# Attention diagonal from products, sample rows in one transpose, last squares by TensorE, conv taps in other proportions

## The chip, the cores and the metric

The kernel runs on one core of a Trainium2 chip. A core has TensorE (PE, with its weight load PEld), VectorE (DVE), ScalarE (ACT), GpSimd (POOL) and SyncE (SP), which issues most of the transfers. The metric is the device time of one launch in microseconds (us).

## What is computed

Two layers of a decoder trunk, for 256 prompt positions and 8 sample positions that share the weights; all in float32.

```python
for l in range(DEPTH):                                  # 2 layers, D_MODEL = 2048
    h = rmsnorm(x, norm_mix[l])
    z = h @ w_in[l]                                     # a_x a_b a_c q k v r lr c_glu d_uv
    ya = a_b * causal_dwconv(a_c * a_x, past_a, conv_a_w)              # 3 taps
    o, S = gla_chunked(q, k, v, log_a, s0)              # gated linear attention, 4 heads
    yb = rms_per_head(o) * gla_norm * silu(r)
    cc = causal_dwconv(c1 * sigmoid(c2), past_c, conv_c_w)             # 31 taps
    yc = silu(layernorm(cc + conv_c_b))
    yd = gelu(u) * (W_s @ layernorm(gelu(vd)) + sg_b)   # chunks of 128 positions
    x = x + concat(ya, yb, yc, yd) @ w_o[l]
    x = x + (silu(n @ w_gate) * (n @ w_up)) @ w_down    # n = rmsnorm(x, norm_ffn[l])
return rmsnorm(x, norm_final), new states

# inside gla_chunked, for positions i >= j of a chunk, b the running sum of log_a:
att[i, j] = sum_d q[i, d] * k[j, d] * exp(b[i, d] - b[j, d])
# on the diagonal the decay is 1:  att[i, i] = sum_d q[i, d] * k[i, d]
```

## The kernel before

All activations are held transposed: features on the partitions, the 264 tokens (256 prompt, 8 sample) along the free side. Every large product goes through `stream` (lines 273 to 324). It reads a weight block of 512 columns in steps of two 128-row tiles. In each step one transfer brings `raw`, ACT rounds it to `wh` (line 293), DVE subtracts to get the remainder `wl` (line 294), and PE makes three products per tile and column group: `wh` by the high half of the activation (line 308), `wh` by its low half (309), `wl` by the high half (310). That is 24 products a step. `wh` and `wl` have three buffers, `raw` four.

The mixer of a layer runs the streams c2, c1, r, q, v, vd, u, ac, ax, ab of eight steps each, then the output projection `w_o` in four streams of eight steps. `w_o` reads the mixed groups in the order of the table at line 829: 12 to 15 (`uu`, spatial gating), 4 to 7 (`rg`, attention), 8 to 11 (`cc`, the conformer conv), 0 to 3 (`ya`, the short conv). Each group has to be rounded to its `yh` (line 382, or 822 for `ya`) and `yl` (383, 823) before PE can use it.

The conformer conv, 31 taps on four tiles of 128 features, doesn't have a place of its own. Its operations (lines 480 to 485, one first tap on ACT and 31 operations on DVE for each tile) come from a generator. After each `wl` of the streams `step_back` (line 250) adds a rate to an account and issues as many as it holds: 1.5 a step for 16 steps, then 2.5 (line 507). When the generator is empty, `fin_c` normalises `cc` and rounds it. A scheduler then fixes the order of the instructions on each engine.

Between q and v the attention is made: the diagonal (lines 563 to 571) as the full 128 by 128 products of keys and queries, from which a predicated copy with the identity mask `idm` takes the diagonal; then seven levels (578 to 604) of decayed blocks, each with a product `ps_lv` and a predicated copy.

At the end, `finish(g, par)` is called after each of the four streams of the last `w_down`. It multiplies by the final gain (`xg`), transposes back to tokens on the partitions, for three token blocks of 128 (the third, tokens 136 to 263, holds the sample's rows in its last eight), adds the squares up in `acc`, and after the last stream takes the sums over the features with `rms_cols` (229), makes the reciprocal root on DVE (`newton`), scales, and writes the results with `dma` on SP.

Of the kernel before, what the change touches and what calls it, by code (L numbers as in the profile page):

```python
# [11 lines left out]
F32 = mybir.dt.float32  # L12
# [3 lines left out]
AF = mybir.ActivationFunctionType  # L16
ALU = mybir.AluOpType

P = 128
D_MODEL = 2048  # L20
KT = D_MODEL // P
NPT = 256
NS = 8
T = NPT + NS
# [21 lines left out]
def hybrid_trunk_kernel(  # L46
# [8 lines left out]
    nc = tc.nc  # L55
# [11 lines left out]
    def psm(name, shape=(P, 512)):  # L67
        t = ps_m.tile([P, 512], F32, tag="m", name=name)
        return t
# [5 lines left out]
    mm = nc.tensor.matmul  # L75
# [10 lines left out]
    nc.gpsimd.memset(ones_g, 1.0 / GW)  # L86
    ones_s = cst.tile([P, P], F32, tag="ones_s", name="ones_s")
    nc.gpsimd.memset(ones_s, 1.0)
    LEVELS = [64, 32, 16, 8, 4, 2, 1]
    idm = cst.tile([P, P], U8, tag="idm", name="idm")  # L90
    smask = cst.tile([P, 4], U8, tag="smask", name="smask")
# [106 lines left out]
    def rstd_cols(cols, n, inv=1.0):  # L198

        hv, y, t = (tmp.tile([P, 12], F32, tag=a, name=a, bufs=2)[:, :n] for a in ("hv", "rs", "nt"))  # L200
        return newton(cols, y, hv, t, inv)
# [27 lines left out]
    def rms_cols(acc):  # L229
        ps = psm("ps_rms")  # L230
        token_means(ps, 0, acc, ones_d)
        return rstd_cols(ps[:, :3], 3)
# [119 lines left out]
    def mixer_phase(l, gain, par, st):  # L352
# [134 lines left out]
        def conv_all():  # L487
            for t in range(4):
                yield from conv_c(t)
# [14 lines left out]
            emit_y(8, cc, tags=("att", "t10"))  # L504

        states_c()
        back.append((conv_all(), fin_c, chain(repeat(1.5, 16), repeat(2.5))))


        rg = mt("rg", [P, 4, T], tag="t4")  # L510
# [46 lines left out]
        def half(r):  # L557
            return slice(r * 64, (r + 1) * 64)

        def blk(Tb):  # L560
            return slice(Tb * P, (Tb + 1) * P)

        for q in range(2):
            for r in range(2):
                pd = psm("ps_dg")
                for Tb in range(2):
                    mm(out=pd[:, blk(Tb)], lhsT=kz[half(r), q, blk(Tb)], rhs=qz[half(r), q, blk(Tb)],
                       start=True, stop=True)
                nc.vector.copy_predicated(
                    out=att[:, 0:2, q, r, :], mask=idm.unsqueeze(1).to_broadcast([P, 2, P]),  # L570
                    data=pd[:, :256].rearrange("p (g i) -> p g i", g=2))

        pma = mt("pm", [P, 4, T])
        pms = [pma[:, 2 * i:2 * i + 2, :NPT] for i in range(2)]
# [251 lines left out]
        win(COL["ab"], 512, ev_ab)  # L826


        order = [o + i for o in (12, 4, 8, 0) for i in range(4)]
        for g in range(4):  # L830
            def ev_o(m, ps, g=g):
                i = 4 * g + m
# [4 lines left out]

    fin = {}

    def fin_tile(g, t, par):  # L840

        if g == 3:
            q = tmp.tile([P, T], F32, tag="t1", name="sqf", bufs=6)
            actf(q, xs[:, 4 * g + t, :], AF.Square)
            tt(out=fin["acc"], in0=fin["acc"], in1=q, op=ALU.add)
        z = tmp.tile([P, T], F32, tag="t1", name="xg", bufs=6)
        ts(out=z, in0=xs[:, 4 * g + t, :], scalar1=par[:, t, ROW["fin"] + g:ROW["fin"] + g + 1],
           scalar2=None, op0=ALU.mult)
        fin.setdefault("xg", []).append(z)

    def finish(g, par):

        if g == 0:
            fin["acc"] = tmp.tile([P, T], F32, tag="acc", name="acc", bufs=1)
            fin["yo"] = act.tile([P, 2, D_MODEL], F32, tag="xl", name="yo")
            fin["ys"] = act.tile([P, D_MODEL], F32, tag="xh", name="ys")
        acc, yo, ys = fin["acc"], fin["yo"], fin["ys"]
        last = g == 3
        if not last:
            add_squares(acc, 2 * g)  # L860
            add_squares(acc, 2 * g + 1)
            for t in range(4):
                fin_tile(g, t, par)
        xg = fin["xg"]
        fin["xg"] = []
        pts = []
        for c in range(3):
            ps = ps_w.tile([P, 512], F32, tag="w", name="ps_y") if last else psm("ps_y")
            for t in range(4):
                transpose(ps[:, t * P:(t + 1) * P], xg[t][:, TOK0[c]:TOK0[c] + P], ident)  # L870
            pts.append(ps)
        if not last:
            for c in range(3):
                dst = yo[:, c, :] if c < 2 else ys
                actf(dst[:, g * 512:(g + 1) * 512], pts[c], AF.Copy)
            return
        y = rms_cols(acc)

        def scaled(c, src, out):
            if c == 1:  # L880
                actf(out, src, AF.Copy, scale=y[:, c:c + 1])
            else:
                ts(out=out, in0=src, scalar1=y[:, c:c + 1], scalar2=None, op0=ALU.mult)

        for c in (0, 1, 2):
            dst = yo[:, c, :] if c < 2 else ys
            for h0, h1 in ((0, 1024), (1024, D_MODEL)):
                if h0:
                    scaled(c, pts[c], dst[:, 1536:])
                hm = min(h1, 1536)  # L890
                scaled(c, dst[:, h0:hm], dst[:, h0:hm])
                if c < 2:
                    dma(out=y_prompt[0, c * P:(c + 1) * P, h0:h1], in_=dst[:, h0:h1])
            if c == 2:
                dma(out=y_sample.rearrange("b s d -> (b s) d"), in_=dst[P - NS:, :])

    def ffn_phase(l, par):
        es = ExitStack()
# [116 lines left out]
```

## Time and profile before

| | us |
|---|---|
| median of 3 runs | 2325.66 (2324.86 to 2325.68) |
| profiled execution | 2325.71 |
| its span, first to last instruction | 2323.8 |
| PE busy | 2293.6 (99%) |
| DVE busy | 1414.0 (61%) |
| ACT busy | 1019.2 (44%) |

The difference between the execution's time and its span, 1.9 us, lies outside the program's instructions. The mean granted clock of TensorE is 0.995 of full speed. The profile's rows name a line, an engine, an operation, and the tiles written and read; buffer numbers are left out. Passes of a float32 product that isn't a transpose appear as two rows each.

### The profile page before, as it was taken

The page shows a single profiled execution, that of the slowest core. Times are in us where ns is not written, and L with a number is a line of the kernel's source. Part 1 is how long each engine was busy: PE and PEld are TensorE (multiplying, and loading weights), DVE is VectorE, ACT ScalarE, POOL GpSimd, SP SyncE. Part 2 cuts the span into 40 slices and gives each one's busy share as a digit, 9 for nine tenths or more (in the row PEclk, how much of TensorE's full clock was granted, in tenths as well). Part 3 has the DMA queues.
Part 4 walks back from the last instruction along what each step waited for, and adds up shares of the span by engine and source line. Part 5 has one row for each costly group of instructions (what it writes and reads, how often), then busy time and mean ns, then how long its engine had stood idle before and what let it go on. Part 6 is the DMA issues. An engine that isn't in the chain of part 4 may idle for free.

```text
span 2323.8 us, 44164 instructions
## 1 busy us (share of the span) xinstructions
PE 2293.6 (99%) x18656; PEld 2271.3 (98%) x18656; DVE 1414.0 (61%) x2076; ACT 1019.2 (44%) x1302; POOL 71.1 (3%) x138
## 2 busy tenths in 40 slices
PE   9999999999999999999999999999999999999997
PEld 8999989999999999999999998999999999999997
DVE  6699966555655555444467998565555555554444
ACT  5644444444444444444345444444444444434333
POOL 3101000000000000000020100000000000000000
PEclk9999999999999999999999999999999999999999
DMA  8446545555555555555574555555555555555553
GB/s 243 146 155 183 172 153 187 182 181 181 180 189 182 182 182 182 179 178 180 182 202 149 174 172 169 162 179 180 181 181 189 182 182 181 182 181 174 177 177 129
DMA packets 208874, 412.44 MB, mean 177 GB/s; under 512 B 14001, under 2 KB 14067, under 8 KB 208644
## 3 DMA queue, kind: packets, MB, share of 16 engines
q1 hardware_dynamic: 204644, 400.53, 54.1%
q0 software_dynamic: 4032, 9.09, 1.5%
q8 instruction: 146, 2.39, 0.4%
q14 instruction: 52, 0.43, 0.1%
HBM read 404.25 MB, written 6.29 MB: 177 GB/s over the span
## 4 chain that ended last, share of the span: by engine, by line
PE 97%; ACT 2%; DVE 0%; issue 0%; DMA 0%; SPq 0%; DVEq 0%; ACTq 0%
PE pw L308 23%; PE pw L309 23%; PE pw L310 23%; PE pwx L308 8%; PE pwx L309 8%; PE pwx L310 8%; PE ps_lv L597 1%; PE ps_os L705 0%; ACT s L701 0%; ACT wh L293 0%; DMA raw<-in_w_in_dram 0%; PE ps_y L870 0%; ACT cc L503 0%; PE ps_sv L774 0%; PE ps_o L667 0%
## 5 line engine op out<-in xcount | busy, mean ns | idle before, releaser
L294 DVE TENSOR_TENSOR wl<-raw,wh 128x1024 fp32r<-128x1024 f32 x752 | 918.8, 1223 | 763.7 <-ACT wh L293 763.0
L293 ACT ACTIVATE wh<-raw 128x1024 fp32r<-128x1024 f32 (+1 forms) x752 | 795.7, 1060 | 1219.5 <-PE pw L309 694.2
L308 PE MATMUL pw<-xh,wh 128*128 128x264 f32 x3136 | 889.4, 286 | 1.9 <-ACT wh L293 1.7
L309 PE MATMUL pw<-xl,wh 128*128 128x264 f32 x3136 | 887.4, 285 | 0.0
L310 PE MATMUL pw<-xh,wl 128*128 128x264 f32 x3136 | 874.0, 285 | 0.1
L308 PEld LDWEIGHTS pw<-xh,wh 128*128 128x128 f32 x3136 | 590.2, 189 | 3.8 <-ACT wh L293 2.4
L309 PEld LDWEIGHTS pw<-xl,wh 128*128 128x128 f32 x3136 | 590.7, 188 | 2.3 <-issue 1.7
L310 PEld LDWEIGHTS pw<-xh,wl 128*128 128x128 f32 x3136 | 583.7, 189 | 6.9 <-issue 4.0
L308 PE MATMUL pwx<-xh,wh 128*128 128x264 f32 x960 | 272.9, 285 | 0.0
L310 PE MATMUL pwx<-xh,wl 128*128 128x264 f32 x960 | 272.2, 284 | 0.0
L309 PE MATMUL pwx<-xl,wh 128*128 128x264 f32 x960 | 272.1, 284 | 0.0
L309 PE MATMUL pw<-hl,wh 128*128 128x264 f32 x880 | 250.6, 285 | 0.0
L308 PE MATMUL pw<-hh,wh 128*128 128x264 f32 x880 | 250.1, 285 | 0.0
L310 PE MATMUL pw<-hh,wl 128*128 128x264 f32 x880 | 248.7, 285 | 0.0
L308 PEld LDWEIGHTS pwx<-xh,wh 128*128 128x128 f32 x960 | 180.8, 188 | 0.1
L310 PEld LDWEIGHTS pwx<-xh,wl 128*128 128x128 f32 x960 | 180.8, 188 | 0.0
L309 PEld LDWEIGHTS pwx<-xl,wh 128*128 128x128 f32 x960 | 180.5, 188 | 0.0
L308 PEld LDWEIGHTS pw<-hh,wh 128*128 128x128 f32 x880 | 165.8, 188 | 0.0
L309 PEld LDWEIGHTS pw<-hl,wh 128*128 128x128 f32 x880 | 165.7, 188 | 0.0
L310 PEld LDWEIGHTS pw<-hh,wl 128*128 128x128 f32 x880 | 165.1, 189 | 0.1
L309 PE MATMUL pwx<-hl,wh 128*128 128x264 f32 x528 | 150.7, 285 | 0.0
L308 PE MATMUL pwx<-hh,wh 128*128 128x264 f32 x528 | 150.2, 285 | 0.0
(311 smaller groups left out, 2259.9 us busy)
## 6 DMA issues: line engine op xcount, KB each, us to landing
raw<-in_w_gate_dram SPq DMA_DIRECT2D x176, 512.0 KB
raw<-in_w_up_dram SPq DMA_DIRECT2D x176, 512.0 KB
raw<-in_w_down_dram SPq DMA_DIRECT2D x176, 512.0 KB
raw<-in_w_in_dram SPq DMA_DIRECT2D x144, 512.0 KB
raw<-in_w_o_dram SPq DMA_DIRECT2D x64, 512.0 KB
raw<-in_w_in_dram SPq DMA_DIRECT2D x16, 528.0 KB
xp<-in_x_prompt_dram SPq DMA_DIRECT2D x4, 512.0 KB
s<-in_state_gla_dram POOLq DMA_DIRECT2D x16, 128.0 KB, 7.9
```

The costliest lines, as they stand in the source:

```text
L293: actf(wh[:, :, :ncol], r[:, :, :ncol], AF.Copy)
L294: sub = tt(out=wl, in0=r[:, :, :512], in1=wh[:, :, :512].bitcast(F32), op=ALU.subtract)
L308: mm(out=o, lhsT=a, rhs=rh[kk], start=first, stop=False)
L309: mm(out=o, lhsT=a, rhs=rl[kk], start=False, stop=False)
L310: mm(out=o, lhsT=wl[:, j, m * P:(m + 1) * P], rhs=rh[kk], start=False, stop=last)
L597: mm(out=pl[:, g * P:(g + 1) * P], lhsT=pm[:, q, blk(Tb)], rhs=qd[:, q, :, Tb * 64:Tb * 64 + 64], start=True, stop=True)
```

## The change

The rates of the conv's operations are 3 a step for eight steps, 2.25 for eight, then 2.5. The projection reads the groups in the order 12, 4, 0, 8. The attention's diagonal is made from a product of queries and keys on DVE (`prod`), summed over each head's 64 features by a narrow product with `ones_r`, and spread by one predicated copy. In `finish` only the two prompt blocks are transposed; the sample's values, 8 tokens by 16 feature tiles, are gathered in one tile `xgs` and transposed once. The squares of the last two tiles are not added on DVE but by products with `one_3` and `ones_d`; for the sample's rows the squares are spread over 16 partitions a token (`accsm`, `sqs`). The results are scaled and written in other pieces.

```diff
@@ -86,6 +86,14 @@
     nc.gpsimd.memset(ones_g, 1.0 / GW)
     ones_s = cst.tile([P, P], F32, tag="ones_s", name="ones_s")
     nc.gpsimd.memset(ones_s, 1.0)
+    one_3 = cst.tile([P, 3], F32, tag="one_3", name="one_3")
+    nc.gpsimd.memset(one_3, 0.0)
+    nc.gpsimd.memset(one_3[:, 0:1], 1.0 / D_MODEL)
+
+    ones_r = cst.tile([P, 2], F32, tag="ones_r", name="ones_r")
+    nc.gpsimd.memset(ones_r, 0.0)
+    for r in range(2):
+        nc.gpsimd.memset(ones_r[r * 64:(r + 1) * 64, r:r + 1], 1.0)
     LEVELS = [64, 32, 16, 8, 4, 2, 1]
     idm = cst.tile([P, P], U8, tag="idm", name="idm")
     smask = cst.tile([P, 4], U8, tag="smask", name="smask")
@@ -504,7 +512,7 @@
             emit_y(8, cc, tags=("att", "t10"))
 
         states_c()
-        back.append((conv_all(), fin_c, chain(repeat(1.5, 16), repeat(2.5))))
+        back.append((conv_all(), fin_c, chain(repeat(3, 8), repeat(2.25, 8), repeat(2.5))))
 
 
         rg = mt("rg", [P, 4, T], tag="t4")
@@ -560,15 +568,16 @@
         def blk(Tb):
             return slice(Tb * P, (Tb + 1) * P)
 
-        for q in range(2):
-            for r in range(2):
-                pd = psm("ps_dg")
-                for Tb in range(2):
-                    mm(out=pd[:, blk(Tb)], lhsT=kz[half(r), q, blk(Tb)], rhs=qz[half(r), q, blk(Tb)],
-                       start=True, stop=True)
-                nc.vector.copy_predicated(
-                    out=att[:, 0:2, q, r, :], mask=idm.unsqueeze(1).to_broadcast([P, 2, P]),
-                    data=pd[:, :256].rearrange("p (g i) -> p g i", g=2))
+        prod = mt("prod", [P, 2, NPT], tag="dd", bufs=2)
+        tt(out=prod, in0=qz[:, :, :NPT], in1=kz[:, :, :NPT], op=ALU.mult)
+        pd = psm("ps_dg")
+        for Tb in range(2):
+            for q in range(2):
+                g = Tb * 2 + q
+                mm(out=pd[:, 2 * g:2 * g + 2], lhsT=prod[:, q, blk(Tb)], rhs=ones_r, start=True, stop=True)
+        nc.vector.copy_predicated(
+            out=att[:, 0:2].rearrange("p s q r i -> p (s q r) i"), mask=idm.unsqueeze(1).to_broadcast([P, 8, P]),
+            data=pd[:, :8].unsqueeze(2).to_broadcast([P, 8, P]))
 
         pma = mt("pm", [P, 4, T])
         pms = [pma[:, 2 * i:2 * i + 2, :NPT] for i in range(2)]
@@ -826,7 +835,7 @@
         win(COL["ab"], 512, ev_ab)
 
 
-        order = [o + i for o in (12, 4, 8, 0) for i in range(4)]
+        order = [o + i for o in (12, 4, 0, 8) for i in range(4)]
         for g in range(4):
             def ev_o(m, ps, g=g):
                 i = 4 * g + m
@@ -837,44 +846,77 @@
 
     fin = {}
 
+    def fin_gain(par, g):
+        return par[:, :, ROW["fin"] + g]
+
+    def spread(a):
+        return a.rearrange("p (s k) -> p s k", s=NS)
+
     def fin_tile(g, t, par):
 
         if g == 3:
             q = tmp.tile([P, T], F32, tag="t1", name="sqf", bufs=6)
             actf(q, xs[:, 4 * g + t, :], AF.Square)
-            tt(out=fin["acc"], in0=fin["acc"], in1=q, op=ALU.add)
+            if t < 2:
+                tt(out=fin["acc"], in0=fin["acc"], in1=q, op=ALU.add)
+            else:
+                qs = tmp.tile([P, T], F32, tag="t1", name="sqs", bufs=6)[:, :P]
+                actf(spread(qs), xs[:, 4 * g + t, NPT:].unsqueeze(2).to_broadcast([P, NS, KT]), AF.Square)
+                fin["sq"].append((q, qs))
         z = tmp.tile([P, T], F32, tag="t1", name="xg", bufs=6)
-        ts(out=z, in0=xs[:, 4 * g + t, :], scalar1=par[:, t, ROW["fin"] + g:ROW["fin"] + g + 1],
+        ts(out=z[:, :NPT], in0=xs[:, 4 * g + t, :NPT], scalar1=fin_gain(par, g)[:, t:t + 1],
            scalar2=None, op0=ALU.mult)
         fin.setdefault("xg", []).append(z)
 
+    def fin_start():
+        fin["sq"] = []
+        fin["acc"] = tmp.tile([P, T], F32, tag="acc", name="acc", bufs=1)
+        fin["yo"] = act.tile([P, 2, D_MODEL], F32, tag="xl", name="yo")
+
+        xh_ = act.tile([P, KT * P], F32, tag="xh", name="xgs")
+        fin["xgs"] = spread(xh_[:, :P])
+        fin["ys"] = xh_[:, P:2 * P]
+
     def finish(g, par):
 
         if g == 0:
-            fin["acc"] = tmp.tile([P, T], F32, tag="acc", name="acc", bufs=1)
-            fin["yo"] = act.tile([P, 2, D_MODEL], F32, tag="xl", name="yo")
-            fin["ys"] = act.tile([P, D_MODEL], F32, tag="xh", name="ys")
-        acc, yo, ys = fin["acc"], fin["yo"], fin["ys"]
+            fin_start()
+        acc, yo, xgs = fin["acc"], fin["yo"], fin["xgs"]
         last = g == 3
         if not last:
             add_squares(acc, 2 * g)
             add_squares(acc, 2 * g + 1)
             for t in range(4):
                 fin_tile(g, t, par)
+        tt(out=xgs[:, :, 4 * g:4 * g + 4], in0=xs[:, 4 * g:4 * g + 4, NPT:].rearrange("p t s -> p s t"),
+           in1=fin_gain(par, g).unsqueeze(1).to_broadcast([P, NS, 4]), op=ALU.mult)
         xg = fin["xg"]
         fin["xg"] = []
-        pts = []
-        for c in range(3):
-            ps = ps_w.tile([P, 512], F32, tag="w", name="ps_y") if last else psm("ps_y")
-            for t in range(4):
-                transpose(ps[:, t * P:(t + 1) * P], xg[t][:, TOK0[c]:TOK0[c] + P], ident)
-            pts.append(ps)
+        pts = [ps_w.tile([P, 512], F32, tag="w", name="ps_y") if last else psm("ps_y") for c in range(2)]
+        for t in range(4):
+            for c in range(2):
+                transpose(pts[c][:, t * P:(t + 1) * P], xg[t][:, c * P:(c + 1) * P], ident)
         if not last:
+            for c in range(2):
+                actf(yo[:, c, g * 512:(g + 1) * 512], pts[c], AF.Copy)
+            return
+
+        ps = psm("ps_rms")
+        accs = tmp.tile([P, T], F32, tag="t1", name="accsm", bufs=6)[:, :P]
+        nc.vector.tensor_copy(spread(accs), acc[:, NPT:].unsqueeze(2).to_broadcast([P, NS, KT]))
+        srcs = [(acc, accs)] + fin["sq"]
+        for i, (src, srcs_) in enumerate(srcs):
             for c in range(3):
-                dst = yo[:, c, :] if c < 2 else ys
-                actf(dst[:, g * 512:(g + 1) * 512], pts[c], AF.Copy)
-            return
-        y = rms_cols(acc)
+                a = src[:, c * P:(c + 1) * P] if c < 2 else srcs_
+                if i == 0 and c == 0:
+
+                    mm(out=ps[:, :3], lhsT=a, rhs=one_3, start=True, stop=False)
+                else:
+                    mm(out=ps[:, c:c + 1], lhsT=a, rhs=ones_d[:, 0:1], start=False,
+                       stop=c == 2 and i + 1 == len(srcs))
+        pss = ps_w.tile([P, 512], F32, tag="w", name="ps_ys")
+        transpose(pss[:, :P], xgs.rearrange("p s k -> p (s k)"), ident)
+        y = rstd_cols(ps[:, :3], 3)
 
         def scaled(c, src, out):
             if c == 1:
@@ -882,17 +924,16 @@
             else:
                 ts(out=out, in0=src, scalar1=y[:, c:c + 1], scalar2=None, op0=ALU.mult)
 
-        for c in (0, 1, 2):
-            dst = yo[:, c, :] if c < 2 else ys
-            for h0, h1 in ((0, 1024), (1024, D_MODEL)):
-                if h0:
-                    scaled(c, pts[c], dst[:, 1536:])
+        for h0, h1 in ((0, 512), (512, 1024), (1024, D_MODEL)):
+            for c in (0, 1):
+                dst = yo[:, c, :]
                 hm = min(h1, 1536)
                 scaled(c, dst[:, h0:hm], dst[:, h0:hm])
-                if c < 2:
-                    dma(out=y_prompt[0, c * P:(c + 1) * P, h0:h1], in_=dst[:, h0:h1])
-            if c == 2:
-                dma(out=y_sample.rearrange("b s d -> (b s) d"), in_=dst[P - NS:, :])
+                if h1 > hm:
+                    scaled(c, pts[c], dst[:, hm:])
+                dma(out=y_prompt[0, c * P:(c + 1) * P, h0:h1], in_=dst[:, h0:h1])
+        scaled(2, pss[:, :P], fin["ys"])
+        dma(out=y_sample.rearrange("b s (k f) -> (b s k) f", f=P), in_=fin["ys"])
 
     def ffn_phase(l, par):
         es = ExitStack()
```

Where the scheduler puts things is shown by the order of instructions of each kernel, at three places in layer 0.

The first is DVE in the first stream of `w_o`: `wl` is a weight split, `L428` (`L436` after) the last normalising step of `cc`, `L383` (`L391`) its `yl`, and `L833` (`L842`) adds the stream's result. Before:

```order
L193 TENSOR_TENSOR sqg<-sqg,rsl 128x264
L194 SCALAR_TENSOR_TENSOR sqg<-sqg 128x264
L195 SCALAR_TENSOR_TENSOR rsl<-sqg,rsl 128x264
L428 TENSOR_TENSOR cc<-cc,rsl 128x1056
L294 TENSOR_TENSOR wl<-raw,wh 128x1024
L383 TENSOR_TENSOR yl_3376<-cc,yh_3375 128x1056
L294 TENSOR_TENSOR wl<-raw,wh 128x1024 x2
L833 TENSOR_TENSOR xs<-xs,pw_3595 128x264
L294 TENSOR_TENSOR wl<-raw,wh 128x1024
```

After:

```order
L203 SCALAR_TENSOR_TENSOR rsl<-sqg,rsl 128x264
L302 TENSOR_TENSOR wl<-raw,wh 128x1024
L832 TENSOR_TENSOR yal<-ya,yah 128x264 x2
L436 TENSOR_TENSOR cc<-cc,rsl 128x1056
L832 TENSOR_TENSOR yal<-ya,yah 128x264
L302 TENSOR_TENSOR wl<-raw,wh 128x1024 x2
L391 TENSOR_TENSOR yl_3126<-cc,yh_3125 128x1056
L302 TENSOR_TENSOR wl<-raw,wh 128x1024 x4
L842 TENSOR_TENSOR xs<-xs,pw_3594 128x264
```

The `yl` of `cc` had two splits behind it before the first result is added; it now has four, and the parts of `ya` (`L832`) stand ahead of it.

The second is DVE at the diagonal in the v stream, with the levels' `dd`, `pm` and `qd` around it. Before (a fourth copy of line 569 follows some rows later):

```order
L591 TENSOR_TENSOR qd<-qk,dd 64x2x128 x4
L589 TENSOR_TENSOR pm<-qk,dd 128x2x2x64
L589 TENSOR_TENSOR pm<-qk,dd 128x2x4x32
L482 SCALAR_TENSOR_TENSOR cc<-cext,par_825,cc 128x256
L569 COPY_PREDICATED att<-idm,ps_dg 128x2x128 x3
L585 TENSOR_TENSOR dd<-bb 128x512 x2
L482 SCALAR_TENSOR_TENSOR cc<-cext,par_825,cc 128x256
L294 TENSOR_TENSOR wl<-raw,wh 128x1024
L484 SCALAR_TENSOR_TENSOR cc<-cext,par_825,accs_866 128x8
```

After:

```order
L302 TENSOR_TENSOR wl<-raw,wh 128x1024
L490 SCALAR_TENSOR_TENSOR cc<-cext,par_832,cc 128x256
L572 TENSOR_TENSOR prod<-qk 128x512
L594 TENSOR_TENSOR dd<-bb 128x512
L490 SCALAR_TENSOR_TENSOR cc<-cext,par_832,cc 128x256 x2
L302 TENSOR_TENSOR wl<-raw,wh 128x1024
L598 TENSOR_TENSOR pm<-qk,dd 128x2x2x64
L490 SCALAR_TENSOR_TENSOR cc<-cext,par_832,cc 128x256
L600 TENSOR_TENSOR qd<-qk,dd 64x2x128 x2
L302 TENSOR_TENSOR wl<-raw,wh 128x1024
L578 COPY_PREDICATED att<-idm,ps_dg 128x1024
L594 TENSOR_TENSOR dd<-bb 128x512
```

Three plus one copies of 256 elements became one of 1024, behind a product of 512, and the first level's `pm` and `qd` moved from ahead of the copies to between product and copy, with two taps of `cc` more around them.

The third is ACT in the q stream, where `absy` belongs to the forget gate. Before:

```order
L293 ACTIVATE wh<-raw 128x2x512
L531 ACTIVATE absy<-ps_pre,par_825 128x264 x2
L532 ACT_TABLE_LOAD
L532 ACTIVATE absy<-absy 128x528
L293 ACTIVATE wh<-raw 128x2x512
L533 ACT_TABLE_LOAD
L533 ACTIVATE absy<-absy 128x528
L293 ACTIVATE wh<-raw 128x2x512
L633 ACT_TABLE_LOAD
L633 ACTIVATE as<-lss 128x16
```

After:

```order
L301 ACTIVATE wh<-raw 128x2x512
L539 ACTIVATE absy<-ps_pre,par_832 128x264 x2
L301 ACTIVATE wh<-raw 128x2x512
L540 ACT_TABLE_LOAD
L540 ACTIVATE absy<-absy 128x528
L541 ACT_TABLE_LOAD
L541 ACTIVATE absy<-absy 128x528
L301 ACTIVATE wh<-raw 128x2x512
L642 ACT_TABLE_LOAD
```

One `wh` moved from between the two table loads to ahead of the first. In layer 1 this place reads as before.

## Rows read from the trace of the kernel before

**Rows 1.** Page, parts 1 and 4: busy us, share, instructions; chain by engine.
```profile
PE 2293.6 (99%) x18656; PEld 2271.3 (98%) x18656; DVE 1414.0 (61%) x2076; ACT 1019.2 (44%) x1302; POOL 71.1 (3%) x138
...
PE 97%; ACT 2%; DVE 0%; issue 0%; DMA 0%; SPq 0%; DVEq 0%; ACTq 0%
```

**Rows 2.** Waits of PE: line, releaser: us in total, times, longest.
```profile
PE pw L308 <- ACT yh L382: 11.1, 2, 5.6
...
PE pw L308 <- ACT wh L293: 1.7, 3, 0.7
```

**Rows 3.** Windows: stretch, us, busy by engine (instructions), PEclk, DMA, GB/s.
```profile
300.92:306.76 5.84, 0.28 (x3) 0.07 (x2) 3.23 (x5) 5.53 (x7) 0.00 (x0) 0.81 0.43 140
306.76:311.30 4.54, 4.50 (x18) 4.19 (x19) 1.24 (x1) 0.00 (x0) 0.00 (x0) 0.50 0.14 53
...
314.00:330.00 16.00, 16.00 (x133) 16.00 (x132) 10.69 (x17) 8.37 (x12) 0.00 (x0) 1.00 0.49 160
```

**Rows 4.** Timeline before the first wait: start, us, engine, line, operation.
```profile
288.88 0.29 PE L308 MATMUL pw<-yh,wh 128*128 128x264 f32 x1
...
291.91 1.11 DVE L823 TENSOR_TENSOR yal<-ya,yah 128x264 fp32r<-128x264 f32 x3
...
305.62 1.08 ACT L382 ACTIVATE yh<-cc 128x1056 fp32r<-128x1056 f32 x1
...
306.74 1.26 DVE L383 TENSOR_TENSOR yl<-cc,yh 128x1056 fp32r<-128x1056 f32 x1 [2.54 <-ACT yh L382]
```

**Rows 5.** Windows of 10 us in layer 0.
```profile
70.00:80.00 10.00, 9.79 (x80) 8.93 (x79) 4.45 (x14) 3.80 (x7) 2.17 (x4) 1.00 0.19 60
...
140.00:150.00 10.00, 10.00 (x86) 10.00 (x86) 9.91 (x18) 3.95 (x7) 0.00 (x0) 1.00 0.46 127
```

**Rows 6.** DVE forms (count; busy us, mean ns), then one split and its reader.
```profile
L482 DVE SCALAR_TENSOR_TENSOR cc<-cext,par,cc 128x256 f32<-128x256 f32 x240 | 113.8, 477 | 1.4
...
L599 DVE COPY_PREDICATED att<-lmask,ps_lv 128x512 f32<-128x512 uint8 x14 | 12.5, 892 | 0.1
...
L569 DVE COPY_PREDICATED att<-idm,ps_dg 128x256 f32<-128x256 uint8 x8 | 3.1, 443 | 0.0
...
L534 DVE TENSOR_TENSOR lsp<-mn,absy 128x512 f32<-128x512 f32 x2 | 1.4, 692 | 0.7 <-ACT absy L533 0.7
...
157.28 1.21 DVE L294 TENSOR_TENSOR wl<-raw,wh 128x1024 fp32r<-128x1024 f32 x1
...
161.17 0.29 PE L310 MATMUL pw<-xh,wl 128*128 128x264 f32 x1
```

**Rows 7.** Timeline of ACT and PE in the q stream.
```profile
102.84 1.28 ACT L532 ACT_TABLE_LOAD   x1
...
103.77 0.28 PE L308 MATMUL pw<-xh,wh 128*128 128x264 f32 x1
...
115.21 1.04 ACT L293 ACTIVATE wh<-raw 128x1024 fp32r<-128x1024 f32 x1
```

**Rows 8.** Chain in order of time: start, us, engine, tile, line, count.
```profile
126.90 1.09 PE ps_dg L567 x12
...
2247.51 0.98 PE ps_y L870 x9
...
2311.81 0.70 PE ps_rms L208 x6
```

**Rows 9.** Timeline at the end, and the window of the output.
```profile
2310.86 0.35 DVE L847 TENSOR_SCALAR xg<-xs,par 128x264 f32<-128x264 f32 x1
...
2314.31 0.75 DVE L883 TENSOR_SCALAR yo<-yo,rs 128x1024 f32<-128x1024 f32 x1
...
2315.09 2.88 SPq L893 DMA_DIRECT2D out_dram<-yo  x4
...
2318.07 1.14 SPq L895 DMA_DIRECT2D out_dram<-ys  x1
...
2315.90:2321.30 5.40, 0.00 (x0) 0.00 (x0) 1.93 (x4) 0.74 (x2) 0.00 (x0) 0.50 1.06 396
```

## Prediction

> **What bounds the kernel now.** I read the page first: TensorE (PE) is busy 99% of the span and carries 97% of the chain that ended last [rows 1]. So only three things can move the time: idle or slow time of PE, its own work, and the stretch at the end when PE is done. I then asked who PE waits for. Apart from the start, two waits matter: `yh` from line 382, 5.6 us at most and twice, once per layer, and short waits for the weight half `wh` [rows 2]. The windows show that the first costs more than it lasts: 5.84 us without products, then 4.54 us in which the granted clock is 0.50 (the 1.2 GHz level) and 18 products run that at the undisturbed pace of 16.00/133 = 0.120 us need 2.2 us [rows 3]. That is 5.7 + 2.4 = 8.1 us in a layer, 16.2 us in both. The timeline tells what was late: the conformer conv `cc`, third of four groups that the output projection reads, gets its `yh` at 305.62 while the projection began at 288.88; `ya`, fourth in the order, was complete at 291.91 + 1.11 = 293.0 [rows 4]. Behind `cc` stands VectorE (DVE): in 140 to 150 us it is busy 9.91 of 10 us, but in 70 to 80 us only 4.45 [rows 5]. It is full late and empty early.
>
> **Taps and projection order.** By the old rates 24 of the conv's 128 operations are due by the end of the q stream and the rest at 2.5 a step, so the last comes in step 58 of the 64 from r to ab. By the new ones 8 × 3 + 8 × 2.25 = 42 are due there, and the end is step 51, seven steps earlier; a step is 24 products of 0.120 us = 2.9 us. The 18 advanced operations cost 18 × 0.48 = 8.6 us of DVE at most [rows 6], and the empty time of the r and q streams has room for them. Besides, `cc` is now read last, two steps = 5.8 us later, and on DVE its `yl` stands two weight splits earlier. Needed was 5.8 us; the two moves give about 20 + 5.8. On ACT the silu and its table load are queued ahead of two `wh`, which have two steps of lead there. What becomes third is `ya`: it was complete 4.1 us after the projection's start and is needed four steps = 11.7 us after it, so 7.6 us to spare. Gain 16.2; from the other side, if `cc` or `ya` is still late by 2 us a layer, without a fall of the clock, 12.
>
> **Diagonal.** Before, PE makes 16 passes of `ps_dg` a layer; 12 of them take 1.09 us, so 1.5 us [rows 8]. After, it makes 8 narrow ones; the nearest row is `ps_rms`, 6 passes of one column in 0.70 us [rows 8], so 0.9 us. DVE loses four predicated copies (4 × 0.44 = 1.8 us) and gains one of 1024 elements, at the rate of line 599 (0.892 us for 512) also 1.8 us [rows 6], and one product of 512, like line 534, 0.7 us. The new copy reads a broadcast from PSUM, which no row shows: without any saving on the overheads of four copies it is 1.8, at half that rate 3.6. It all falls in the stretch where DVE is full. Near its end a split is done at 157.28 + 1.21 = 158.5 and PE reads it at 161.17 [rows 6], 2.7 us of lead, so PE's 0.6 us may partly return as a wait for `wl`. I take 0.4 a layer, 0.8 together; ends: 1.2 gained, 2 lost.
>
> **A moved split.** In layer 0 the q stream's fourth `wh` comes off the place behind the exponential's table load and stands ahead of it. There it waits for its buffer, free when PE ends the step at 103.77, and all that ACT does next (two tables, a `wh`, sixteen state scalings) is queued behind it. The next `wh`, at 115.21, is the one for which PE already waits [rows 2, 7]. Where ACT went on at 102.84 [rows 7] it now idles until the buffer is free, so all behind is 0.9 us later, and the wait grows by 0.9. If ACT has slack that I don't see, 0. In layer 1 that place is unchanged.
>
> **Sample rows.** Each of the first three `finish` calls makes 8 transposes for 12. Nine took 0.98 us [rows 8], so 4 × 0.109 × 3 = 1.3 us off PE; if they hide in the stream's own weight loads, 0.5. Three ACT copies go, three small DVE products come; both engines wait in that stage.
>
> **The end.** The sum of squares no longer passes DVE for the last two tiles, but TensorE takes 9 products instead of 3. They queue behind a DVE copy that follows the last `xg` (2310.86 + 0.35) [rows 9], so they start near 2311.2, and 14 passes of 0.117 us end at 2312.8, 0.3 us later than 2312.5 now. The first scaling is 512 wide instead of 1024, 0.3 us shorter: the first output issue stays at 2315.1. From there the end is a transfer: 2 MB at 396 GB/s take 5.3 us [rows 9], and they do not shrink. Only the sample's last one does: eight rows of 8 KB follow the others now, 128 rows of 512 B then, and DVE has 128 columns to scale for it instead of 2048. I take 0.7 gained. If the narrow products hide in the transposes, 1.5 gained; if the longer row of issues shows, 1 lost.
>
> The transfer is where a rule speaks against the change. The Trainium skill ("DMA: Bandwidth & Descriptors", Rules for kernel authors) says to coalesce many small transfers, those under 64 KB being mostly overhead; the output goes from five transfers to seven here. This trace has 2.88 us for four issues, and data flowing without a gap behind them, so a further issue would have a price only where SP falls behind. With the fixed cost of about 2 us that the same page gives (Anatomy of one DMA), for another issuing path, each of the two more would bring the sum to about 2311.6 in all, an estimate.
>
> **Sum.** The profiled execution took 2325.71 us (span 2323.8), 0.05 above the median of the runs, 2325.66. 2325.7 − 16.2 − 0.8 + 0.9 − 1.3 − 0.7 = 2307.6 us.
>
> **Rivals.**
> 1. The wait moves to the weight splits. The taps sit denser, and the attention's levels now stand one to three steps later on DVE and ACT. For it speaks that DVE is full in 140 to 150 us; against it that the early stretch has idle time and the operations per step from v on are still 2.5. If PE waits for 13 of the 18 taps in each layer, 2 × 13 × 0.40 (their spacing; 0.48 with the overlap) = 10.3 us come back: 2318. Chance 0.12.
> 2. The extra issues show at the end. For it: the issues of the last kind took 1.14 us against 0.72 as a mean of the four before [rows 9]; against: data flows behind them at a full rate. Two more at 1.14 instead of my gain of 0.7: 2307.6 + 0.7 + 2.3 = 2310.6. Chance 0.10.
> 3. The change doesn't do what it says: the projection still waits as long, for `ya` or `cc`. Then only the small terms are left: 2325.7 − 1.9 = 2323.8. For it only that the wait has ended on a long chain of DVE, ACT and PE before; against, 7.6 us and more to spare. Chance 0.03.
> 4. Slower: the broadcast predicated copy is far slower than its neighbours. It holds DVE's queue, `wl` behind it, and PE; after each wait of some 5 us the clock falls [rows 3]. To eat 18 us it must hold PE 9 us in each layer, which with 2 us of lead is about 13 us for 1024 elements, seven times the rate of line 599. Beyond it, at 15 us, 2 × 2 us more: 2330. Chance 0.02.
>
> My own forecast has 0.70; its own range, from the ends of its terms, is 2304.5 to 2311.5. The remaining 0.03 is a larger gain, if the emptier DVE also removes waits for `wh` or for `wl`: 2303.
>
> **Range and chances.** Rival 2 lies inside, half of rival 1 is taken in: 2304 to 2315. A run of this kernel can be told from no change at about 0.2%, 4.65 us, so faster means under 2321.0: all but rivals 3 and 4, 0.95. Within: 0.03. Slower: 0.02.
>
> **What would show it.** Right: no wait of PE for line 391 (old 382), clock 1.00 right through both output projections, DVE busier than 4.45 us in 70 to 80 us; PE's wait for `wh` in the q stream of layer 0 about 0.9 us longer than in layer 1; `ps_y` with 8 transposes; the last output landing some 0.7 us sooner after the last product. Wrong: a PE wait for `wl`, `prod` or `pm` in the v stream, a predicated copy of over 4 us, or a stretch at 0.50 in the middle of the run.

## The result, and the profile after

| | before | after |
|---|---|---|
| median of 4 runs | 2325.67 us (2324.86 to 2327.01) | 2311.38 us (2310.46 to 2312.69) |
| profiled execution | 2325.71 | 2310.46 |
| its span | 2323.8 | 2308.3 |

The ratio is 0.9938, with a 95% interval of 0.9921 to 0.9956: 14.3 us faster. The forecast was 2307.6, a gain of 18.1; the median lies at the upper edge of the forecast's own range. The page of the kernel after, parts 1 and 4:

```profile
PE 2287.1 (99%) x18637; PEld 2266.1 (98%) x18637; DVE 1415.0 (61%) x2074; ACT 1018.4 (44%) x1302; POOL 71.5 (3%) x143
...
PE 93%; issue 3%; ACT 1%; DVE 1%; DMA 0%; POOL 0%; SPq 0%; ACTq 0%; DVEq 0%; POOLq 0%
```

PE has lost 6.5 us of busy time and the span 15.5 us, so more than half of the gain is idle time that is gone. The waits of PE (line, releaser: us in total, times, longest), beside [rows 2]:

```profile
PE ps_x L351 <- DMA xp<-in_x_prompt_dram: 5.7, 1, 5.7
PE pw L316 <- ACT wh L301: 2.9, 3, 1.9
PE pw L318 <- DVE wl L302: 1.8, 2, 1.1
PE pw L316 <- DVE uext L806: 0.3, 1, 0.3
```

The wait for `yh` is not there. The longest wait for `wh` has become 1.9, and two kinds of wait on DVE are new. The windows over the output projection of layer 0, with the columns of [rows 3]:

```profile
286.52:304.00 17.48, 17.48 (x146) 17.48 (x145) 13.11 (x21) 11.76 (x16) 0.00 (x0) 1.00 0.51 157
304.00:316.00 12.00, 12.00 (x101) 12.00 (x100) 7.67 (x11) 5.72 (x8) 0.00 (x0) 1.00 0.78 240
```

PE is busy throughout and the clock stays at 1.00, where it had stood idle for 5.84 us and run 4.54 us at 0.50. Layer 1 shows the same (1421.6 to 1450 us, clock 1.00).

A ledger tells where the rest went. Both kernels make the same 18,112 weight products (the products of `stream`) in nearly the same order, so I took the start of the product with the same number in both traces. The numbers are chosen where the other passes of PE so far are the same in both, but for those that the change takes away. In the feed-forward streams, which the change doesn't touch, the difference between these two traces stays constant to 0.04 us, and between any two of the kept traces to 0.1. The last column is what the stretch itself adds to the difference.

| weight product | what lies between it and the one above | start before, after | difference | added |
|---|---|---|---|---|
| 744 | start, c2, c1, r, most of q | 114.44, 114.65 | +0.21 | +0.2 |
| 768 | one step of q, with the wait for `wh` | 118.66, 120.00 | +1.35 | +1.1 |
| 1296 | v, vd, half of u, with the attention, layer 0 | 203.00, 203.08 | +0.08 | −1.3 |
| 2016 | rest of u, ac, ax, ab, start of the projection | 297.13, 298.23 | +1.10 | +1.0 |
| 2304 | output projection, where it had waited | 340.40, 333.34 | −7.06 | −8.2 |
| 10368 | rest of layer 0; layer 1 to half of u, with the attention | 1348.39, 1340.02 | −8.37 | −1.3 |
| 11064 | rest of u to ab, start of the projection, layer 1 | 1439.60, 1433.27 | −6.33 | +2.0 |
| 11280 | output projection, layer 1 | 1473.99, 1459.63 | −14.36 | −8.0 |
| 18100 | rest of layer 1, to the last `w_down` with the sample rows | 2308.07, 2292.70 | −15.36 | −1.0 |
| end of span | the end | 2323.8, 2308.3 | −15.5 | −0.1 |

Against the forecast's terms: the wait gave 16.2, as said. The diagonal gave 2.5, not 0.8. The moved split cost 1.1, not 0.9. The sample rows gave 1.1, not 1.3 (the 1.0 of the last stage holds a drift of 0.1 from earlier). The end gave 0.1, not 0.7. And the stretches from u to the start of the projection lost 3.0 us that the sum does not have.

What is late there? On PE's side in layer 1, the waits in the window 1390 to 1425:

```profile
PE pw L318 <- DVE wl L302: 1.1, 1, 1.1
PE pw L316 <- DVE uext L806: 0.3, 1, 0.3
```

The other wait for `wl`, of 0.7 us, is in layer 0. Counted from product to product beside the undisturbed pace, the three cost 0.8, 0.5 and 1.3 us: 2.6 of the 3.0. And DVE at the same place in layer 0 (timeline: start, us, engine, line, operation):

```profile
262.19 1.23 DVE L302 TENSOR_TENSOR wl<-raw,wh 128x1024 fp32r<-128x1024 f32 x1 [3.84 <-ACT wh L301]
263.70 0.69 DVE L786 TENSOR_TENSOR sv<-ps_sv,sgb 128x512 f32<-128x512 f32 x1 [0.28 <-PE ps_sv L783]
...
266.65 1.25 DVE L422 TENSOR_TENSOR cc<-cc,ps_mu 128x1056 f32<-128x1056 f32 x1
...
272.57 1.25 DVE L391 TENSOR_TENSOR yl<-uu,yh 128x1056 fp32r<-128x1056 f32 x1
273.74 0.87 DVE L820 SCALAR_TENSOR_TENSOR ya<-uext,par,ya 128x256 f32<-128x256 f32 x2
274.53 1.22 DVE L302 TENSOR_TENSOR wl<-raw,wh 128x1024 fp32r<-128x1024 f32 x1
```

DVE has been idle for 3.84 us before the first row, and then the spatial gating (`sv`, `yl` of `uu`), the normalising of `cc` and the short conv (`ya`) all come at once; the `wl` at 274.53 stands behind them and PE waits for it.

### The profile page after: what moved, and what is told of

Same layout as the page of the kernel before. It is cut to its first block, busy times and chain, and to the rows that moved or that the text cites. A ratio compares the mean times of both kernels' runs of the same rounds, so it can differ in the third digit from the quotient of the medians.

```text
span 2308.3 us, 44137 instructions
## 1 busy us (share of the span) xinstructions
PE 2287.1 (99%) x18637; PEld 2266.1 (98%) x18637; DVE 1415.0 (61%) x2074; ACT 1018.4 (44%) x1302; POOL 71.5 (3%) x143
## 4 chain that ended last, share of the span: by engine, by line
PE 93%; issue 3%; ACT 1%; DVE 1%; DMA 0%; POOL 0%; SPq 0%; ACTq 0%; DVEq 0%; POOLq 0%
PE pw L318 22%; PE pw L316 22%; PE pw L317 22%; PE pwx L316 8%; PE pwx L317 8%; PE pwx L318 8%; PE ps_lv L606 1%; ACT s L710 0%; ACT wh L301 0%; DVE wl L302 0%; DMA raw<-in_w_in_dram 0%; PE ps_os L714 0%; PE ps_y L898 0%; DMA vb<-vsd 0%; PE ps_x L351 0%
```

## Experiments

All ran beside the kernel before, whose medians were 2325.67 to 2326.36.

**Which edit removes the wait.** Three kernels, each the kernel before with:

```diff
rates, rates_order:
-        back.append((conv_all(), fin_c, chain(repeat(1.5, 16), repeat(2.5))))
+        back.append((conv_all(), fin_c, chain(repeat(3, 8), repeat(2.25, 8), repeat(2.5))))
order, rates_order:
-        order = [o + i for o in (12, 4, 8, 0) for i in range(4)]
+        order = [o + i for o in (12, 4, 0, 8) for i in range(4)]
```

Rates alone:

> Before with the new tap rates alone. Theory A (the wait is removed by the earlier taps; the late weight splits of the changed kernel at the ac and ax streams need the longer chain of the new diagonal as well): no PE wait for yh of cc, granted clock 1.00 in both output projections, -16.2; the wh split moved ahead of the table load makes the wait of layer 0 in the q stream about 2.0 us instead of 0.9, +1.1; no PE wait for wl near 275 and 1410 us. 2325.7 - 15.1 = 2310.6 us. Theory B (the denser taps alone make the weight splits late): the same, and PE waits for wl of 0.8 us in layer 0 and 1.3 us in layer 1 at those places: 2313. Theory C (the new order is needed): part of the yh wait stays: above 2315.

Order alone:

> Before with the new order of the projection's groups alone. Theory A (the wait was 5.84 us, two steps are 5.85 us): yh of cc comes about when it is needed, 0 to 1 us of wait for yh or yl is left in each layer, no fall of the clock; wh wait in the q stream 0.9 us in both layers, no wl waits: 2325.7 - 16.2 + (0 to 2) = 2309.5 to 2311.5. Theory B (the parts of ya now stand ahead of cc on DVE and make it later): 2 us or more of wait a layer and a fall of the clock behind it: 2314 to 2320.

Both:

> Before with both, the old diagonal and the old end. Theory A: as with the rates alone, 2310.6, since the wait is gone with either; no wl waits near 275 and 1410 us. Theory B (denser taps make the splits late): wl waits of 0.8 and 1.3 us there, 2313.

Measured: rates 2311.56 (2311.06 to 2312.37, ratio 0.994), order 2312.65 (2311.94 to 2313.70, 0.9945), both 2311.61 (2311.34 to 2312.47, 0.994). Either edit alone removes nearly all of it. With the rates `cc` is rounded eleven microseconds before it is read (its `yh`, then the first product of the projection's third group, weight product 2048):

```profile
290.46 1.07 ACT L382 ACTIVATE yh<-cc 128x1056 fp32r<-128x1056 f32 x1
...
302.59 0.28 PE L308 MATMUL pw<-yh,wh 128*128 128x264 f32 x1
```

With the order alone it is just late, and PE waits half a microsecond a layer; in the ledger 1.5 us of the 8.1 are left in each layer, the rest of them in short gaps right behind the wait. PE's waits in that kernel:

```profile
PE pw L308 <- ACT wh L293: 2.1, 5, 0.7
PE pw L308 <- ACT yh L382: 1.1, 2, 0.6
```

The waits are those of theory A in all three, and there is no wait for `wl`: denser taps alone do not make the splits late. The medians lie about 1 us above theory A's figures. For the rates the ledger has 14.9 us of the 15.1 between products 744 and 18100, so there the mechanism is whole; for the order alone 1.5 us a layer are left where theory A allowed 1. The `wh` of 1.9 us comes with the rates, and only with them. The surprise is that rates alone are as fast as the whole change: diagonal, sample rows and the end together were worth nothing that the medians show.

**The diagonal.** First alone on the kernel before, then the changed kernel with the old diagonal put back (the hunk at line 563 of the diff, one way and the other).

Alone:

> Before with the new diagonal alone. Theory A (the two traces: PE is 1.27 us further ahead behind the attention in each layer): -2.5, the yh wait as long as before: 2323.2. Theory B (the prediction's 0.4 a layer): 2324.9. Theory C (its longer chain makes the work behind it on DVE later, cc among it): yh waits longer than 5.6 us, 2326 or more.

Put back:

> The changed kernel with the old diagonal put back. Theory A (the late weight splits at 275 and 1410 us come from the new diagonal and the new rates together: the diagonal's longer chain brings the spatial gating's sums to step 73, the rates bring the conv's normalising to the same steps): no PE wait for wl there; 1.3 us a layer of PE are lost again, 0.9 and 2.1 us of waits go; the end and the sample rows as in the changed kernel: about 2311.4 + 2.5 - 3.0 = 2310.9, no worse than the changed kernel. Theory B (the splits are late by the rates, the diagonal is a plain gain): the waits stay, 2313.9.

Alone it took 2327.56 (2324.29 to 2329.81 in 10 runs, ratio 1.0007, interval 0.9998 to 1.0016): there is no gain, as theory C says. Its waits:

```profile
PE pw L312 <- ACT yh L386: 13.4, 2, 6.7
...
PE ps_sta L808 <- DVE uext L802: 0.9, 2, 0.6
PE pw L314 <- DVE wl L298: 0.5, 2, 0.3
```

The wait for `yh` grew from 11.1 to 13.4, and `uext` and `wl` are new. With the old diagonal the changed kernel took 2309.91 (2309.71 to 2310.68, 0.9931), and there is no wait for `wl` (theory A). So the new diagonal is the cause of those waits, though the ledger shows 1.3 us a layer less of PE.

The median is 1.5 us under that of the changed kernel, but the intervals of the two ratios overlap, and that the diagonal is worth as much is not shown. By the ledger, between products 744 and 18100, the old diagonal is 1.3 us slower; this one execution had a fall of the clock behind the `wh` wait of 1.9 us, which ends at 117.12, and it cost 1.5 us (from product 744 to 1296, against the rates alone, which have the same diagonal). Windows with the columns of [rows 3], with the old diagonal put back:

```profile
115.00:118.00 3.00, 1.11 (x9) 0.89 (x9) 0.90 (x1) 3.00 (x9) 0.00 (x0) 1.00 0.17 65
118.00:120.00 2.00, 1.97 (x11) 1.76 (x11) 1.93 (x4) 2.00 (x3) 0.00 (x0) 0.68 0.24 24
120.00:122.00 2.00, 2.00 (x11) 2.00 (x10) 2.00 (x4) 0.37 (x2) 0.00 (x0) 0.50 0.71 251
```

The profile of the rates alone has the same wait and 1.00 in these windows. Without the fall the two diagonals, waits included, are 0.2 us apart by the ledger, the old one ahead.

Why would a diagonal made in 8 passes instead of 16 delay what follows? The changed kernel on DVE, at the diagonal:

```profile
127.06 0.68 DVE L572 TENSOR_TENSOR prod<-qk 128x512 f32<-128x512 f32 x1
127.66 0.68 DVE L594 TENSOR_TENSOR dd<-bb 128x512 f32<-128x512 f32 x1
...
133.42 1.32 DVE L578 COPY_PREDICATED att<-idm,ps_dg 128x1024 f32<-128x1024 uint8 x1
134.64 0.67 DVE L594 TENSOR_TENSOR dd<-bb 128x512 f32<-128x512 f32 x1
```

`prod` has the tag `dd` with two buffers, the same two in which each level's `dd` rotates. While `prod` holds one, only one level can be ahead, not two. The levels slip, then the attention, then the gating's sums `ps_sv`, which start at 253.0 before and at 262.6 after. I gave `prod` another buffer, one that `lsp` uses before it and `ke` after it:

```diff
-        prod = mt("prod", [P, 2, NPT], tag="dd", bufs=2)
+        prod = mt("prod", [P, 2, NPT], tag="t10")
```

> The changed kernel with one edit: prod has another buffer (the one that lsp has used before and ke uses after), not one of the two of the levels' dd. Theory A (the diagonal's chain is longer because prod takes a dd buffer, so that only one level's dd can stand ahead of the copy; that delays the attention by three steps and brings the spatial gating's sums and the conv's normalising together at step 73): the gating's sums come back to step 69, no PE wait for wl or uext near 270 and 1405 us, PE's 1.27 us a layer stay gained; wh wait of 2 us in layer 0 stays: 2311.4 - 3.0 = 2308.4. Theory B (the chain is longer by its own steps on DVE, PE and DVE): waits of 0.8 and 1.7 us stay, 2311.

It took 2307.91 (2307.67 to 2308.55, ratio 0.9921, interval 0.9905 to 0.9938): theory A. The same place on DVE, and PE's waits in that kernel:

```profile
129.57 0.69 DVE L571 TENSOR_TENSOR prod<-qk 128x512 f32<-128x512 f32 x1
...
132.38 1.28 DVE L593 TENSOR_TENSOR dd<-bb 128x512 f32<-128x512 f32 x2
...
135.12 1.32 DVE L577 COPY_PREDICATED att<-idm,ps_dg 128x1024 f32<-128x1024 uint8 x1
```

```profile
PE ps_x L350 <- DMA xp<-in_x_prompt_dram: 5.6, 1, 5.6
PE pw L315 <- ACT wh L300: 2.9, 3, 1.9
```

Two `dd` stand ahead of the copy again, `ps_sv` starts at 249.5, and the waits for `wl` and `uext` are gone. Between products 744 and 11064 this kernel gains 3.0 us on the changed one, the size of the loss. The diagonal itself kept its 1.3 us a layer.

**The old rates with everything else.**

> The changed kernel with the old rates put back. Theory A: no wh wait beyond 0.9 us in the q stream of layer 0; at steps 73 to 77 about 0.9 us of waits a layer, as with the diagonal alone; cc, which was 6.86 us late with the diagonal alone, is read 5.85 us later, so 1 us late and 1.5 us with what follows, no fall of the clock: 2327.6 - 2 x (6.86 + 2.4 - 2.4) - 1.3 = 2312.6. Theory B (cc is later again because ya's parts stand ahead of it): yh wait over 2 us and a fall of the clock, 2316 or more.

It took 2318.66 (2317.7 to 2319.38, 0.9968). That is theory B's size, for another reason. ACT in front of the projection's last group:

```profile
305.08 1.28 ACT L510 ACT_TABLE_LOAD   x1
306.37 2.10 ACT L510 ACTIVATE cc<-cc,par 128x264 f32<-128x264 f32 x4
308.38 1.04 ACT L300 ACTIVATE wh<-raw 128x1024 fp32r<-128x1024 f32 x1
309.33 1.07 ACT L389 ACTIVATE yh<-cc 128x1056 fp32r<-128x1056 f32 x1
```

The silu of the late `cc` stands ahead of the next weight split, so PE waits 2.5 us for `wh` and then 0.5 for `yh`, and the clock falls behind it:

```profile
306.50:310.00 3.50, 1.03 (x7) 0.61 (x5) 0.55 (x1) 3.50 (x6) 0.00 (x0) 1.00 0.52 159
310.00:315.00 5.00, 4.43 (x22) 4.13 (x23) 1.85 (x2) 0.39 (x1) 0.00 (x0) 0.66 0.32 111
```

With the delayed attention the faster rates are needed; with the old one the order nearly sufficed.

**Rates in between.** The rates `repeat(1.75, 16), repeat(2.5)`, with the new order and end: they leave ACT's place in the q stream as before. With the old diagonal, the new one, and the new one with `prod` in the other buffer (own buffer, below):

> Before with the new order, the new end and sample rows, the old diagonal, and rates between the two: 1.75 a step for 16 steps, then 2.5; the place in ACT's q stream is the old one. Theory A: cc comes 4 to 5 us earlier than with the order alone, no wait for yh; wh waits of 0.9 us in both layers as before; no wl waits: 2325.7 - 16.2 - 1.3 = 2308.2. Theory B (DVE has no room in the v stream): some wl waits and a part of the yh wait stay, 2310 to 2312.

> The same with the new diagonal. Theory A (the diagonal gives 1.27 us a layer and its later chain costs 0.9 us a layer at steps 73 to 77): 2308.2 - 0.7 = 2307.5, with waits of PE for uext and wl there. Theory B (the diagonal's gain stands when nothing else crowds DVE there): no such waits, 2305.7. Theory C (crowding as in the changed kernel): 2309 or more.

> The same buffer, and rates of 1.75 a step for 16 steps, then 2.5 (the kernel with these rates and the old diagonal took 2308.26, with the new diagonal and the dd buffer 2310.62). Theory A: the new diagonal's 1.27 us a layer without its waits, 2308.3 - 2.5 = 2305.8; no wait for yh, wl or uext, 0.9 us for wh in each layer. Theory B: the diagonal's gain is eaten whatever the buffer, 2308.3 or more.

Measured: 2308.26 (2307.81 to 2310.93, 0.9925), 2310.62 (2310.18 to 2310.97, 0.9933) and 2306.70 (2306.61 to 2309.17, 0.9918). The first is theory A to 0.1 us. The second is theory C, and the waits are `yl`, `yh` and `wl` (1.4, 1.0 and 0.5 us). The third has theory A's waits, and its ledger gains 1.3 us a layer at the diagonal; its median is 0.9 above the expectation. Its profiled run was the one at 2309.17: against the version with two pieces below, the same program up to the end, it was 2.9 us late when the second stream began (product 192) and hardly more at the last `w_down`.

**The end.** Two kernels, each the last one (mild rates, new diagonal, own buffer) with:

```diff
two pieces:
-        for h0, h1 in ((0, 512), (512, 1024), (1024, D_MODEL)):
+        for h0, h1 in ((0, 1024), (1024, D_MODEL)):
squares on DVE:
-            if t < 2:
+            if t < 4:
                 tt(out=fin["acc"], in0=fin["acc"], in1=q, op=ALU.add)
```

> As the one before, but each prompt block's output in two pieces of 1024 columns as before, five issues for seven. Theory A (the transfer of 2 MB bounds the end and an earlier first piece is worth its 0.3 us): first issue 6.3 us after the last weight product's start for 6.05, the end 0.2 to 0.4 us later. Theory B (the two more issues cost their time): the end 0.5 us or more sooner.

> As the second, but the squares of the last two tiles are added on DVE as before and no products take them. Theory A (the fourteen narrow passes behind the last tile made hv start 0.6 us later than before, 3.75 for 3.15 us after the last weight product's start): the products end at 3.0 to 3.2 us for 3.72, the first issue at 5.4 to 5.5, the end 0.5 to 0.6 us sooner. Theory B (the adds on DVE delay the last transposes and the sums as much): no difference within 0.1 us.

Measured 2306.14 (2305.98 to 2306.45, 0.9913, interval 0.9899 to 0.9928) and 2306.30 (2305.52 to 2307.50, 0.9914). Since the start differs between runs by more than this, I compare the end by the trace, from the start of the last weight product:

| us after the last weight product's start | before | after | mild rates, own buffer | two pieces | squares on DVE |
|---|---|---|---|---|---|
| last product ends | 3.10 | 3.72 | 3.72 | 3.72 | 3.20 |
| first output issue | 5.69 | 6.04 | 6.04 | 6.31 | 5.53 |
| last output issue | 8.66 | 9.24 | 9.24 | 9.29 | 8.72 |
| end of span | 14.40 | 14.27 | 14.28 | 14.04 | 13.76 |

In the kernel after, the copy of `acc`, the last products, the first step that reads them, and the issues:

```profile
2295.75 0.23 DVE L906 COPY accsm<-acc 128x128 f32<-128x128 f32 x1
...
2297.40 0.36 PE L915 MATMUL ps_rms<-ones_d,sqs 128*128 128x1 f32 x2
2297.80 0.16 DVE L194 TENSOR_SCALAR hv<-ps_rms 128x3 f32<-128x3 f32 x1 [1.81 <-PE ps_rms L915]
...
2300.08 3.11 SPq L934 DMA_DIRECT2D out_dram<-yo  x6
...
2303.28 1.14 SPq L936 DMA_DIRECT2D out_dram<-xgs  x1
```

With the squares added on DVE the same steps come half a microsecond sooner after the last product (at 2290.02), and so does the end: theory A, as expected.

```profile
2293.25 0.16 DVE L193 TENSOR_SCALAR hv<-ps_rms 128x3 f32<-128x3 f32 x1 [0.66 <-PE ps_rms L914]
...
2295.54 3.10 SPq L933 DMA_DIRECT2D out_dram<-yo  x6
```

DVE waited 1.81 us for the products that replaced its adds; with the adds it waits 0.66. The two pieces start 0.27 us later and end 0.24 us sooner, which is neither expectation: the direction of theory B, half its size. And it is not shown that the issues are the reason, since kernels with the same end differ by as much: from the last weight product to the end it is 14.03 with the old diagonal put back into the changed kernel, for 14.27, and 14.10 with the new diagonal alone, for 14.40 before. The version with two pieces has the lowest median of all, 20.2 us under the kernel before beside it where the changed kernel was 14.3 under. Both edits together were not run.

## Why the forecast was right, and where it was not

- **The wait and the clock.** Right in mechanism and size: 8.2 and 8.0 us for 8.1 a layer. The forecast added the 20 us of the rates to the 5.8 of the order without asking whether one would do. The rates alone did. Its signs came true: no wait for line 391, clock 1.00 in both projections, and DVE busy 6.81 us in 70 to 80 us. "Empty early" was read from that one window; 60 to 70 us had 8.26 and 80 to 90 us 8.98 of 10 us, and the room was in 90 to 120 us, with 19.98 of 30.
- **The diagonal.** Two errors of opposite sign. Its PE time was mis-sized: the sum took 1.5 us for the 16 old passes, from the 12 that had a row [rows 8], and 0.9 for the new ones, which took 0.8; the old ones cost 2.1, since the other four stood in a group with 16 passes of the levels and cost more each than the twelve: from product to product the twelve add 1.3 us, and that group adds 2.6 where 16 such passes without them add 1.8. And the predicted return "as a wait for `wl`" came in another stage, through a buffer that the forecast had not looked at. The rows of DVE's order ahead of the prediction hint at it: a pair of `dd` stands behind the old copies, a single one on each side of the new copy. The predicated copy with a broadcast source took 1.32 us, under the lower bound of 1.8. The forecast's ends for this term were 1.2 gained and 2 lost; 2.5 gained and 3.0 lost make 0.5 lost, which lies between them by luck.
- **The moved split.** Right in mechanism: PE waits 1.9 us in layer 0 and 0.7 in layer 1, and it goes with the rates. What it left out is that the longer wait can bring down the clock, which cost 1.5 us more in one profiled execution.
- **Sample rows.** Right but for 0.2: 1.1 us.
- **The end.** The step that failed is the start of the last products: `hv` was forecast 0.3 later and came 0.6 later, in the main since the copy of `acc` itself, 0.23 us on DVE, was put at nothing, and the first issue came 0.35 later where none was forecast. The six issues took 0.23 longer than the four had. The 0.7 did come, from the last issue to the end (5.74 us before, 5.03 after), but the last issue itself is 0.58 later.
- **Rivals.** Rival 1 (waits move to the weight splits) happened in part, with 3.0 us for its 10.3 and in a later stream. Of its two reasons the later levels held; the denser taps did not, as the rates alone show. It was counted as excluding the forecast, when part of it could be added. Rival 2 (issues at the end) is small: two issues fewer went with 0.24 us. The Trainium skill's rule to coalesce small transfers ("DMA: Bandwidth & Descriptors", Rules for kernel authors) names those under 64 KB, and the prompt's pieces here have 256 KB and more; no run here shows its gain. By the fixed cost of about 2 us that the Trainium skill gives ("DMA: Bandwidth & Descriptors", Anatomy of one DMA) for another issuing path, the two more would have cost about 4 us, an estimate; the trace doesn't agree, with 0.24. Rivals 3 and 4 did not occur.

Without the 3.0 us of waits and the 0.6 at the end the profiled execution would have taken 2306.9, 0.7 under the forecast. That it came within 2.9 us of the forecast with them is luck in part: the 1.7 us that PE saved on the diagonal beyond its term hid more than half of the waits. It was the fastest of the four runs, 0.9 under their median; the others have no trace, so where they lost it stays open (the start and the clock, below, are likely places).

## What to carry to other kernels

Ask of each new temporary which buffers it rotates in and who else waits for them; a two-deep ring with a third user turns an overlap into a chain, and the cost appears stages later. When two edits aim at one wait, test each alone. Compare traces by the start of the same product, since medians here can't see a microsecond and the ledger can; but look first whether one of the traces holds an event of its own, as the fall of the clock at 118 us was.

## What was not expected of the hardware

- A narrow pass cost as much as a wide one here. These are rows of the chain in the kernel after (eight passes of 2 columns) and of its timeline (eight of 128):

```profile
130.66 0.79 PE ps_dg L577 x8
```

```profile
134.92 1.05 PE L606 MATMUL ps_lv<-qd,pm 128*128 128x128 f32 x8
```

The two durations are taken in different ways; from the weight product before to the one after (130.38 to 131.31, and 134.80 to 135.73) each group adds 0.81 us to the stream's pace. The Trainium skill says that loading weights takes time by their columns ("TensorE: Matmul & The Clock Gate", LDWEIGHTS (loading the stationary operand)), and both load 128; the trace agrees, with 0.10 us a pass at either width. No run here varies the columns that are loaded.
- The same wait brought the clock down in one execution and not in another. PE waited 1.9 us for `wh` at 117 us with the rates alone, and the clock stayed at 1.00; it waited as long with the old diagonal put back, and the clock was at 0.50 (the 1.2 GHz level) from 118.7 to 122.1 us. Behind the waits of 2.5 and 0.5 us with the old rates it fell in both layers. The five kernels with the wait of 1.9 us have 20 runs; the mean granted clock is 0.997 in one run of each and 0.998 in the others, and in four of the five that run is the longest. All 26 runs with the order alone or the rates in between have 0.998. Only one trace shows the place, so for the other four runs it is likely and not shown.
- The start differs between the profiled executions, each of another kernel, by up to 3.7 us (the first product of the sixth step at 31.96 in one, 35.68 in another, where the first weights come), while the feed-forward streams that they have in common agree to 0.1 us afterwards. The spread of a kernel's runs, 0.5 to 3 us for most, would fit that; only the profiled runs show it.
